# Attention scores of two heads beside each other on half arrays, three products a head, in place of two stacked whole-array products a head

## The chip, the cores and the metric

The kernel runs on one core of a Trainium2 chip. The metric is the device time of one execution in microseconds (us). The time before is 1629.16 us, the median of three runs (1628.31 to 1630.95). In the text, TensorE (PE in the profile, PEld for its weight loads) multiplies matrices, VectorE (DVE) and ScalarE (ACT) do elementwise work, GpSimd (POOL) helps, and SyncE (SP) issues most DMAs.

## The reference

A trunk of two layers over 512 latent tokens (a grid of 8 rows by 64 columns) and 256 context tokens, width 1024, all in float32. Each layer has an attention sub-layer and a SwiGLU sub-layer (hidden width 2816), each with a modulated RMSNorm ahead and a gated residual add behind. Layer 0 has four differential heads (each the difference of two softmaxes over all 768 keys) and eight neighbourhood heads (a window of the grid plus all context keys, with a bias). Layer 1 has 16 query heads on four key heads, with a window of 128 to each side, all context keys, and one learned sink logit a head. A head has 64 dimensions. What the change touches is the score computation, which in all of them has this core:

```python
s = jnp.einsum('bqhd,bnhd->bhqn', q, k).astype(jnp.float32) * (HEAD_DIM ** -0.5)
p = jax.nn.softmax(s, axis=-1)
...
o = jnp.einsum('bhqn,bnhd->bqhd', p.astype(v.dtype), v)
```

Context tokens go through the same layers but attend to context keys only; the second layer gives latent tokens alone.

## The kernel before

**Precision.** To keep float32 accuracy with TensorE's faster single-pass type (fp32r), every large operand is split into a high part, rounded to fp32r, and a low part, the rest. A projection (`mm3`, L205 to L210) makes three products: high by high, high by low, low by high. The projections, the two SwiGLU sub-layers and the scores work so; transposes and the product of probabilities and values (called PV here) use plain float32.

**Scores.** Two heads are handled as a pair; a projection leaves their 2 x 64 dimensions on 128 partitions. A head needs a sum over 64 partitions only, so `evac_pair` (L364) lays a head out on all 128: for head j it writes the high part to the head's own 64 partitions and the low part to the other 64. ScalarE makes the two high parts (L369), VectorE the two low ones (L372), each with 64 partitions. `swap_halves` (L386) makes by two DMAs a second copy `k2` of the keys with the halves exchanged. A whole-array product of q with `k1` then gives high by high plus low by low, and one with `k2` gives the two mixed terms: two products a head, each of 128 rows.

**Stages.** The differential heads are units u = 0 to 3 (`diff_steps`, L788), the neighbourhood heads units 4 to 7 (`na_steps`, L885). Each unit has four steps of 128 latent queries and one for the 256 context queries (`softmax_ctx`, L763). Score products are L804 and L805 (256 and 512 key columns), L912 and L914 (256 and 256) and, for context queries, L769 and L770 (256 each). The grouped-query stage of layer 1 has eight head pairs with four query blocks each (`gqa_step`, L1462); its products are L1477 (256 context keys) and L1479 (256 or 384 window keys). Behind the scores come, for each head, a minimum along the keys on VectorE (L806, L772, L915, L1481; the queries carry a factor of -0.125, so the minimum plays the maximum's part), the exponential on ScalarE (L808, L777, L922, L1486), a division by the sum (L782, L1494 and others), transposes on TensorE (L821, L935, L1503), copies out of PSUM, and PV (L825, L946, L1517). PV of the neighbourhood and of the grouped-query heads writes two heads to 64 columns of the array each, so that it shows as 128*64.

**PSUM.** It has eight banks. In layer 0's attention four belong to the score tiles (two tiles of two banks, `sps`), two to projections (`linp`) and two to transposes and PV (`tp`); in layer 1's attention four to scores, one to projections, three to the rest. A differential or a grouped-query step takes one score tile for each of its two heads; a neighbourhood step and a context step take one tile for both.

**Order.** `run_steps` (L406) issues a step's scores and softmax (`a`), then the transposes and PV of the step before (`b`), then a few fillers: projections for the next unit, the values, loads and low-rank sums for the modulation, and at the end first parts of the output projection. This is only a priority: the program is built with a scheduler that simulates the engines and orders each engine's instructions anew, earlier ones in the text first where they are ready. On the chip each engine runs its queue in that order. The keys' copies `k2` go through SP's queue, where the weight loads stand too (L131, L142), and `k2` has one buffer in layer 0, so that the swap of one unit waits for the last score products of the unit before.

Of the kernel before, what the change touches and what calls it, by code (L numbers as in the profile page):

```python
# [8 lines left out]
F32 = mybir.dt.float32  # L9
# [23 lines left out]
def f32(ap):  # L33
    return ap.bitcast(F32)
# [3 lines left out]
def tile_trunk(  # L38
# [325 lines left out]
    def evac_pair(dst, col, n, src, scale):  # L364

        c = slice(col, col + n)
        for j in range(2):
            a = slice(64 * j, 64 * j + 64)
            nc.scalar.activation(dst[a, j, c], src[a, :], AF.Copy, scale=scale)  # L369
        for j in range(2):  # L370
            a, o = slice(64 * j, 64 * j + 64), slice(64 - 64 * j, 128 - 64 * j)
            nc.vector.scalar_tensor_tensor(  # L372
                dst[o, j, c], src[a, :], scale, f32(dst[a, j, c]), op0=ALU.mult, op1=ALU.subtract
            )
# [220 lines left out]
    with ExitStack() as st:  # L595
        sps = st.enter_context(tc.tile_pool(name="a_s", bufs=2, space=PSUM, reuse_waits="tile"))
# [4 lines left out]
        sp2 = lambda shape=(P, 1024): sps.tile(list(shape), F32, tag="s", name="s")  # L601
# [30 lines left out]
        with ExitStack() as s0:  # L632
# [27 lines left out]
            psv = [sp2((P, 2, 512)) for _ in range(2)]  # L660
# [48 lines left out]
        def qk_tiles(u):  # L709
            units[u] = {  # L710
                "k": sp.tile([P, 2, NT], F32R, tag="k1", name="k1"),
                "k2": sp.tile([P, 2, NT], F32R, tag="k2", name="k2", bufs=1),
# [11 lines left out]
        def qk_c(u, key, w):  # L724
# [38 lines left out]
        def softmax_ctx(u):  # L763

            q, k1, k2 = (units[u][z] for z in ("q", "k", "k2"))
            s = sp2((P, 2, 2, 256))
            for c in range(2):
                for i in range(2):
                    nc.tensor.matmul(s[:, c, i, :], q[:, c, i * P : (i + 1) * P], k1[:, c, 0:256], start=True, stop=False)  # L769
                    nc.tensor.matmul(s[:, c, i, :], q[:, c, i * P : (i + 1) * P], k2[:, c, 0:256], start=False, stop=True)  # L770
            nm, rs = small("nm4", 4), small("rs4", 4)
            nc.vector.tensor_reduce(nm, s.rearrange("p a b n -> p (a b) n"), axis=AX.X, op=ALU.min)  # L772
# [15 lines left out]
        def diff_steps(u):  # L788
# [4 lines left out]
            def x_step(i):  # L793
                d = {}

                def a():
                    q, k1, k2 = (units[u][z] for z in ("q", "k", "k2"))
# [1106 lines left out]
```

## Time and profile before

| | |
|---|---|
| median of three runs | 1629.16 us |
| the profiled execution, its own time | 1634.54 us |
| its span, first to last instruction | 1632.7 us |
| mean granted TensorE clock | 0.992 |
| matmuls and weight loads | 10222 each |
| HBM read and written | 160.45 MB and 4.86 MB |

The profile shows one execution, and the lines that matter stand in the prediction. A line of a group gives the line of the kernel, the engine, the operation, the tiles it writes and reads, the shape, the count, then busy time in all and the mean duration of one in ns, then the idle time ahead of it and what ended it. A shape such as 128*64 behind a matmul is the part of the array it uses, rows by columns. In a timeline the first number is the start, the second the duration of the merged piece, and x2 says that two instructions of a kind were merged. Matmuls are pipelined, so that one's duration overlaps the next one's; the pace is read from start to start. In the sums by stage each engine has its busy time and count of instructions.

### The profile page before, as it was taken

Reading aid. Unit: us, or ns where it says so; the run is one execution under the profiler, and the core shown is the slowest. Engines: PE = TensorE matmul, PEld = TensorE weight load, DVE = VectorE, ACT = ScalarE, POOL = GpSimd, SP = SyncE. Lnnn points to the kernel's source line nnn. Section 1 sums busy time; section 2 is a strip of 40 time slices with the busy share of each in tenths; the row PEclk is TensorE's granted clock in tenths of the full one; section 3 lists DMA queues with packets and bytes.
Section 4 is the critical chain, followed back from the end, with each engine's and each line's share of the span. In section 5 each row is a group of like instructions: output and inputs, shape, how many; then the busy total and the mean of one; then the engine's idle time right before and its main releaser. Section 6 shows DMA issues by size and latency. Waiting matters only on the chain.

```text
span 1632.7 us, 26333 instructions
## 1 busy us (share of the span) xinstructions
PE 1569.6 (96%) x10222; PEld 1403.5 (86%) x10222; DVE 1255.6 (77%) x2157; ACT 747.0 (46%) x1324; POOL 267.0 (16%) x311
## 2 busy tenths in 40 slices
PE   5899998998999999999999999999999999999997
PEld 3798887886878899999999998887788899989897
DVE  4757698976688888978899867787665887869686
ACT  4446554555334532432424244456655542524344
POOL 2222222345010000010100011264322000000001
PEclk9999999999999999999999999999999999999999
DMA  9322244544235365576766753311010442323321
GB/s 343 98 57 85 89 149 129 186 139 132 72 109 154 95 183 158 152 197 168 195 180 169 211 134 95 104 53 40 14 40 27 152 132 66 125 82 104 117 78 52
DMA packets 69220, 198.48 MB, mean 122 GB/s; under 512 B 6900, under 2 KB 19348, under 8 KB 69096
## 3 DMA queue, kind: packets, MB, share of 16 engines
q1 hardware_dynamic: 59464, 164.40, 31.7%
q0 software_dynamic: 9056, 31.87, 9.1%
q8 instruction: 81, 1.33, 0.3%
q10 hardware_dynamic: 576, 0.52, 0.1%
q14 instruction: 43, 0.35, 0.1%
HBM read 160.45 MB, written 4.86 MB: 101 GB/s over the span
## 4 chain that ended last, share of the span: by engine, by line
PE 64%; DVE 7%; DMA 4%; issue 2%; ACT 2%; POOL 0%; DVEq 0%; SPq 0%; ACTq 0%; POOLq 0%
PE f L1272 5%; PE f L1274 5%; PE f L1273 5%; PE f L1685 4%; PE f L1684 4%; PE f L1683 4%; PE f L1313 3%; PE f L1314 3%; PE f L1315 3%; PE t L1517 2%; PE lin L207 2%; PE lin L208 2%; PE lin L209 2%; PE f L1737 2%; PE f L1736 2%; PE f L1738 2%
## 5 line engine op out<-in xcount | busy, mean ns | idle before, releaser
L196 ACT ACTIVATE wh<-raw 128x1024 fp32r<-128x1024 f32 (+1 forms) x96 | 92.3, 978 | 233.7 <-DVE raw L507 115.8
L207 PE MATMUL lin<-hb,wh 128*128 128x512 f32 (+1 forms) x456 | 162.8, 358 | 8.2 <-DVE q L372 2.2
L208 PE MATMUL lin<-hb,wh 128*128 128x512 f32 (+1 forms) x456 | 160.3, 352 | 0.5 <-DVE hb L197 0.4
L209 PE MATMUL lin<-hb,wl 128*128 128x512 f32 (+1 forms) x456 | 158.9, 348 | 0.0
L197 DVE TENSOR_TENSOR wl<-raw,wh 128x1024 fp32r<-128x1024 f32 (+1 forms) x96 | 106.8, 1119 | 34.9 <-ACT wh L196 32.9
L269 DVE SCALAR_TENSOR_TENSOR junk<-raw,tables 128x1024 bf16<-128x1024 f32 x80 | 97.7, 1222 | 20.2 <-DMA raw<-in_ada_wT_dram 19.9
L202 POOL DMA_DIRECT2D wl<-raw x39 | 34.1, 873 | 444.1 <-ACT wl L201 393.8
L207 PEld LDWEIGHTS lin<-hb,wh 128*128 128x128 f32 x456 | 86.4, 190 | 23.4 <-issue 4.5
L1313 PE MATMUL f<-g,wh 128*128 128x512 f32 (+1 forms) x304 | 102.8, 339 | 1.2 <-DVE q L1298 0.7
L1314 PE MATMUL f<-g,wh 128*128 128x512 f32 (+1 forms) x304 | 102.7, 339 | 0.0
L1684 PE MATMUL f<-hb,wh 128*128 128x256 f32 x360 | 101.7, 283 | 0.0
L1683 PE MATMUL f<-hb,wh 128*128 128x256 f32 x360 | 101.4, 283 | 0.0
L1685 PE MATMUL f<-hb,wl 128*128 128x256 f32 x360 | 101.2, 283 | 0.0
L1315 PE MATMUL f<-g,wl 128*128 128x256 f32 (+1 forms) x304 | 100.8, 336 | 0.0
L158 ACT CAST wh<-raw 128x1024 fp32r<-128x1024 f32 x61 | 63.9, 1047 | 77.9 <-PE lin L208 24.0
L1272 PE MATMUL f<-hb,wh 128*128 128x384 f32 x288 | 96.4, 335 | 0.9 <-ACT q L1259 0.9
L159 DVE TENSOR_TENSOR wl<-raw,wh 128x1024 fp32r<-128x1024 f32 x61 | 79.8, 1309 | 22.6 <-ACT wh L158 22.4
L208 PEld LDWEIGHTS lin<-hb,wh 128*128 128x128 f32 x456 | 86.7, 190 | 12.2 <-issue 0.9
L1274 PE MATMUL f<-hb,wl 128*128 128x384 f32 x288 | 96.3, 334 | 0.0
L1273 PE MATMUL f<-hb,wh 128*128 128x384 f32 x288 | 96.2, 334 | 0.0
L209 PEld LDWEIGHTS lin<-hb,wl 128*128 128x128 f32 x456 | 86.6, 190 | 10.4 <-issue 0.3
L339 POOL TENSOR_TENSOR ns_a<-ns_a,ns_s 128x256 f32<-128x256 f32 (+1 forms) x16 | 16.2, 1013 | 435.2 <-ACT ns_s L335 435.2
(395 smaller groups left out, 4948.7 us busy)
## 6 DMA issues: line engine op xcount, KB each, us to landing
raw<-in_w_dram SPq DMA_DIRECT2D x132, 512.0 KB, 3.7
raw<-in_ada_wT_dram SPq DMA_DIRECT2D x80, 512.0 KB, 4.2
wl<-raw POOLq DMA_DIRECT2D x39, 512.0 KB, 5.9
raw<-in_w_ab_dram SPq DMA_DIRECT2D x24, 512.0 KB, 4.2
raw<-in_ada_w_dram SPq DMA_DIRECT2D x16, 512.0 KB, 9.5
k<-k SPq DMA_DIRECT2D x16, 384.0 KB, 5.8
raw<-in_w_c_dram SPq DMA_DIRECT2D x12, 512.0 KB, 3.6
nb<-in_na_bias_dram POOLq DMA_DIRECT2D x16, 256.0 KB, 3.6
```

The lines of the kernel that those rows point to most:

```text
L207: nc.tensor.matmul(ps, wh(k), xh(k), start=k == 0, stop=False)
L208: nc.tensor.matmul(ps, wh(k), xl(k), start=False, stop=False)
L209: end = nc.tensor.matmul(ps, wl(k), xh(k), start=False, stop=k == n - 1)
L1272: nc.tensor.matmul(ps, wh(k), b[:, 0, :], start=k == 0, stop=False)
L1273: nc.tensor.matmul(ps, wh(k), b[:, 1, :], start=False, stop=False)
L1274: nc.tensor.matmul(ps, wl(k), b[:, 0, :], start=False, stop=k == 3)
L1313: nc.tensor.matmul(ps, hi, g[:, 0, cols[v]], start=first, stop=False)
L1314: nc.tensor.matmul(ps, hi, g[:, 1, cols[v]], start=False, stop=False)
L1315: nc.tensor.matmul(ps, lo, g[:, 0, cols[v]], start=False, stop=last)
L1683: nc.tensor.matmul(ps, wh(k), b[:, 0, :], start=k == 0, stop=False)
L1684: nc.tensor.matmul(ps, wh(k), b[:, 1, :], start=False, stop=False)
L1685: nc.tensor.matmul(ps, wl(k), b[:, 0, :], start=False, stop=k == 3)
```

## The change

- `evac_pair` writes the high part of both heads into one plane of the tile and the low part into another, all 128 partitions in one instruction on each engine. A head's high and low parts now lie on the same 64 partitions.
- A new helper, `scores`, takes three products for each head (high by high, high by low, low by high), each over the 64 partitions of that head. The two heads' products alternate: head 0 on rows 0 to 63 of the array, head 1 on rows 64 to 127. From the second product on, each is ordered behind the one before on TensorE and has a high priority in the scheduler.
- Layer 0 has no `k2` and no `swap_halves` any more. In layer 1 `k2` stays, because both query heads of a pair use the same key head, which must lie on both halves.
- The differential steps and the context steps of units 0 to 3 use one score tile of four banks for both heads (`sp4`); from unit 4 on the pool is replaced by the former two tiles of two banks (`sp2`). The grouped-query stage has one tile of four banks instead of two of two.
- A scratch tile of a later norm, which lay in `k2`'s place, has a tag of its own.

```diff
     def evac_pair(dst, col, n, src, scale):
         c = slice(col, col + n)
-        for j in range(2):
-            a = slice(64 * j, 64 * j + 64)
-            nc.scalar.activation(dst[a, j, c], src[a, :], AF.Copy, scale=scale)
-        for j in range(2):
-            a, o = slice(64 * j, 64 * j + 64), slice(64 - 64 * j, 128 - 64 * j)
-            nc.vector.scalar_tensor_tensor(
-                dst[o, j, c], src[a, :], scale, f32(dst[a, j, c]), op0=ALU.mult, op1=ALU.subtract
-            )
+        nc.scalar.activation(dst[:, 0, c], src, AF.Copy, scale=scale)
+        nc.vector.scalar_tensor_tensor(dst[:, 1, c], src, scale, f32(dst[:, 0, c]), op0=ALU.mult, op1=ALU.subtract)
+
+    def head(t, c):
+        return t[64 * c : 64 * c + 64]
+
+    def scores(*groups):
+        last = None
+        for outs, qs_, ks_ in groups:
+            for n, (a, b) in enumerate(((0, 0), (0, 1), (1, 0))):
+                for o, q, k in zip(outs, qs_, ks_):
+                    with tc.issue_after(last.ins) if last else nullcontext(), tc.high_priority() if last else nullcontext():
+                        last = nc.tensor.matmul(o, q(a), k(b), start=n == 0, stop=n == 2)
...
-        sps = st.enter_context(tc.tile_pool(name="a_s", bufs=2, space=PSUM, reuse_waits="tile"))
...
-        sp2 = lambda shape=(P, 1024): sps.tile(list(shape), F32, tag="s", name="s")
+        dst_ = st.enter_context(ExitStack())
+        dps = dst_.enter_context(tc.tile_pool(name="a_s", bufs=1, space=PSUM, reuse_waits="tile"))
+        sp4 = lambda: dps.tile([P, 2, 1024], F32, tag="s", name="s")
+        sps = []
+
+        def sp2(shape):
+            if not sps:
+                dst_.close()
+                sps.append(st.enter_context(tc.tile_pool(name="n_s", bufs=2, space=PSUM, reuse_waits="tile")))
+            return sps[0].tile(list(shape), F32, tag="s", name="s")
...
-                "k2": sp.tile([P, 2, NT], F32R, tag="k2", name="k2", bufs=1),
...
-            if key == "k":
-                swap_halves(units[u]["k2"], dst)
-            elif u >= 4:
+            if key == "q" and u >= 4:
...
-                    for c in range(2):
-                        s = sp2()
-                        for lo, n, at_ in ((256, 256, 0), (512, 512, 256)):
-                            nc.tensor.matmul(s[:, lo : lo + n], q[:, c, qc : qc + P], k1[:, c, at_ : at_ + n], start=True, stop=False)
-                            nc.tensor.matmul(s[:, lo : lo + n], q[:, c, qc : qc + P], k2[:, c, at_ : at_ + n], start=False, stop=True)
+                    both = sp4()
+                    both = [both[:, c] for c in range(2)]
+                    scores(*[(
+                        [s[:, lo : lo + n] for s in both],
+                        [lambda a, t=t: t[:, a, qc : qc + P] for t in qh],
+                        [lambda b, t=t, cs=slice(at_, at_ + n): t[:, b, cs] for t in kh],
+                    ) for lo, n, at_ in ((256, 256, 0), (512, 512, 256))])
+                    for c, s in enumerate(both):
...
-        sps = st.enter_context(tc.tile_pool(name="g_s", bufs=2, space=PSUM, reuse_waits="tile"))
+        sps = st.enter_context(tc.tile_pool(name="g_s", bufs=1, space=PSUM, reuse_waits="tile"))
...
-                for c in range(2):
-                    ql = q[:, c, i * P : (i + 1) * P]
-                    s = sps.tile([P, 1024], F32, tag="s", name="s")
-                    for n, k in ((0, k1), (1, k2)):
-                        nc.tensor.matmul(s[:, 256:512], ql, k[:, kv, 0:NC], start=(n == 0), stop=(n == 1))
-                    for n, k in ((0, k1), (1, k2)):
-                        nc.tensor.matmul(s[:, 512 : 512 + nk], ql, k[:, kv, NC + lo * P : NC + lo * P + nk], start=(n == 0), stop=(n == 1))
+                both = sps.tile([P, 2, 1024], F32, tag="s", name="s")
+                both = [both[:, c] for c in range(2)]
+                ql = [lambda a, t=head(q, c): t[:, a, i * P : (i + 1) * P] for c in range(2)]
+                kh = [head((k1 if kv % 2 == c else k2)[:, kv // 2], c) for c in range(2)]
+                cs = slice(NC + lo * P, NC + lo * P + nk)
+                scores(
+                    ([s[:, 256:512] for s in both], ql, [lambda b, t=t: t[:, b, 0:NC] for t in kh]),
+                    ([s[:, 512 : 512 + nk] for s in both], ql, [lambda b, t=t: t[:, b, cs] for t in kh]),
+                )
+                for c, s in enumerate(both):
```

The neighbourhood and the context steps change in the same way, with `scores` for their products.

More of the change, by code (lines that the diff above doesn't have):

```diff
@@ L1 @@
-from contextlib import ExitStack
+from contextlib import ExitStack, nullcontext
 import concourse.bass as bass
@@ L659, in tile_trunk @@
             psk, psq = linp(), linp()
-            psv = [sp2((P, 2, 512)) for _ in range(2)]
+            psv = sp4().rearrange("p c (t n) -> p c t n", t=2)
+            psv = [psv[:, t] for t in range(2)]
             wv = [tuple(wslice(t, 256) for t in wv)]
@@ L796, in a @@
                 def a():
-                    q, k1, k2 = (units[u][z] for z in ("q", "k", "k2"))
+                    qh, kh = ([head(units[u][z], c) for c in range(2)] for z in ("q", "k"))
                     qc = NC + i * P
@@ L1419, in k_x @@
             mm3(ps, *w, xh, xl)
-            evac_pair(k1[:, 2 * i : 2 * i + 2, :], NC, NX, rope_of(ps, gp), 1.0)
+            evac_pair(k1[:, i], NC, NX, rope_of(ps, gp), 1.0)
         def k_c(i, w):
```

44 lines of the change are left out of this document (22 added, 22 removed).

## Prediction

> **What bounds the kernel now.** I read the page first, then the sums by stage, then TensorE's timeline and the waits where the scores are computed.
>
> ```profile
> span 1632.7 us, 26333 instructions
> PE 1569.6 (96%) x10222; PEld 1403.5 (86%) x10222; DVE 1255.6 (77%) x2157; ACT 747.0 (46%) x1324; POOL 267.0 (16%) x311
> ...
> PE 64%; DVE 7%; DMA 4%; issue 2%; ACT 2%; POOL 0%; DVEq 0%; SPq 0%; ACTq 0%; POOLq 0%
> ```
>
> TensorE is busy for 96% of the span and makes 64% of the chain that ended last. The change lies in three stages, which by their first and last score products reach about from 75 to 257 us (differential heads), to 430 us (neighbourhood heads) and from 1055 to 1260 us (grouped-query heads); the sums over them:
>
> ```profile
> core 0: us, PE busy (x) PEld busy (x) DVE busy (x) ACT busy (x) POOL busy (x), PEclk, DMA share, GB/s
> 75.00:257.00 182.00, 175.26 (x1183) 159.20 (x1182) 133.80 (x213) 96.70 (x205) 38.64 (x38) 1.00 0.31 94
> 257.00:430.00 173.00, 164.18 (x1147) 138.85 (x1148) 129.58 (x248) 87.57 (x212) 67.94 (x94) 0.97 0.48 144
> 1055.00:1260.00 205.00, 200.09 (x1503) 161.68 (x1502) 141.00 (x329) 119.08 (x314) 77.00 (x82) 1.00 0.12 36
> ```
>
> TensorE idles 7, 9 and 5 us there; VectorE is at 74, 75 and 69%. So what counts is what TensorE's own queue gets longer or shorter, and only then its waits. Busy time of a matmul overlaps its neighbour's, so I take the pace from start to start:
>
> ```profile
> 1187.60 0.39 PE L209 MATMUL lin<-hb,wl 128*128 128x512 f32 x1
> 1187.83 0.39 PE L207 MATMUL lin<-hb,wh 128*128 128x512 f32 x1
> 1188.05 0.40 PE L1477 MATMUL s<-gk,gq 128*128 128x256 f32 x2
> 1188.29 0.40 PE L1479 MATMUL s<-gk,gq 128*128 128x256 f32 x2
> 1188.53 0.40 PE L208 MATMUL lin<-hb,wh 128*128 128x512 f32 x1
> 1188.76 0.40 PE L209 MATMUL lin<-hb,wl 128*128 128x512 f32 x1
> 1189.09 0.43 PE L1517 MATMUL t<-pt,gv 128*64 128x128 f32 x2
> 1189.45 0.50 PE L1477 MATMUL s<-gk,gq 128*128 128x256 f32 x2
> 1189.79 0.39 PE L1479 MATMUL s<-gk,gq 128*128 128x256 f32 x2
> 1190.11 1.09 PE L1517 MATMUL t<-pt,gv 128*64 128x128 f32 x14
> 1191.13 1.09 PE L1503 MATMUL t<-ident,p 128*128 128x128 f32 x8
> 1191.98 0.48 PE L207 MATMUL lin<-hb,wh 128*128 128x512 f32 x1
> ```
>
> Three prices come out. A product of 512 columns takes 0.23 us (1187.60 to 1187.83), one of 256 takes 0.12 (two from 1188.05 to 1188.29); 384 lies halfway, 0.175. The PV products (L1517) use half the array's columns each, two heads beside each other: 14 of them, the drain behind them included, start to next start 1.02 us, 73 ns each, while the eight whole-array transposes (L1503) with the same 128 moving columns take 0.85 us, 106 ns each. So two halves of the array do run at the same time, here halves of columns. And a change of that shape costs: L209 to L1517 takes 0.33 where 0.23 is the pace; the pair behind L1517 takes 0.34 (1189.45 to 1189.79) where 0.24 is the pace; L1479 to L1517 takes 0.32 instead of 0.24. I read 0.1 us for draining and another 0.1 for a first weight load that nothing covers, where the next operand is a large one.
>
> **The products.** Per 256 or 512 key columns, the two heads had four whole-array products; they get three pairs on halves of rows. If a pair runs as one product does, a quarter goes. Their counts:
>
> ```profile
> L1479 PE MATMUL s<-gk,gq 128*128 128x384 f32 x64 | 16.8, 341 | 0.0
> L912 PE MATMUL s<-k,q 128*128 128x256 f32 x64 | 15.5, 316 | 3.0 <-DMA k<-k 2.3 <-issue 0.4 <-ACT p L922 0.2
> L804 PE MATMUL s<-k,q 128*128 128x512 f32 x32 | 12.8, 399 | 0.0
> ...
> L769 PE MATMUL s<-k,q 128*128 128x256 f32 x32 | 8.7, 300 | 0.7 <-ACT p L808 0.6
> ```
>
> Each line stands for one of the two products of a head (L805, L914 and L770 are the second ones; L1477 and L1479 hold both), so there are 16 differential steps, 16 neighbourhood steps, 8 context steps and 32 grouped-query steps, half of these with 384 columns and half with 256. Before, a differential step is 4 x 0.12 + 4 x 0.23 = 1.40 us: a quarter is 0.35, times 16 is 5.6. A neighbourhood, context or short grouped-query step is 8 x 0.12 = 0.96: 0.24, times 40 is 9.6. A long grouped-query step is 0.48 + 0.70 = 1.18: 0.295, times 16 is 4.7. Sum **-19.9 us**. No row shows half arrays of rows: if the two halves ran one after the other it would be 12 products for 8, 79.6 x 0.5 = +39.8 us. I take the first, because the nearest row (L1517) shows two halves at once.
>
> **The changes of shape.** 72 score blocks (16 + 16 + 8 + 32) become stretches with another shape than the projections and transposes around them, two sides each. In the stretch above, one block lies between projections and the other between two PV runs, where a change is paid already; I take a third of the 104 sides of the 52 blocks beside PV work as paid, so 144 - 35 = 109 sides are new. At 0.2 us where a projection follows and 0.1 to 0.15 where a transpose with its smaller load does, I take 0.15: **+16 us**. Bounds: 0, if the row form needs no drain, and 144 x 0.2 = +29 if no block shares a side. "TensorEngine Tiling (Array Packing)" of the Trainium skill, section Tiling Modes, says that changing the tiling mode, not just the tile, drains TensorE. The gaps at L1517 agree for columns; the page gives no price, and no run here shows it for rows: by the rule the sum below stands, without it it falls by these 16 us.
>
> **The second copy of the keys.** In layer 0 every head pair sent its keys through two SP transfers to get them with halves swapped, and there is one such buffer: the transfer starts when the last scores of the pair before are done.
>
> ```profile
> 377.43 0.13 PE s L770
> ...
> 377.58 0.46 SPq L387
> ...
> 378.09 6.46 DMA k<-k
> ...
> 384.69 0.36 PE s L912
> ```
>
> ```profile
> PE lin L207 <- DVE q L372: 2.2, 1, 2.2
> ...
> PE s L805 <- DMA k<-k: 1.7, 1, 1.7
> ...
> PE s L912 <- DMA k<-k: 2.3, 2, 1.6
> ```
>
> Here the chain of waits runs through the copy, 377.58 to 384.69, while TensorE finds other work for part of it; its idle time that ended with the copy is 1.7 + 2.3 = 4.0 us. These waits go, and with them two places for each of eight head pairs in SP's queue, behind which weight loads stood. I take **-5 us**, between 4.0 and 7.1; what comes next there are the loads of the head outputs for the output projection. The four swaps of the grouped-query keys stay, of the same size.
>
> **Splitting whole.** evac_pair issues one instruction on ScalarE and one on VectorE instead of two each.
>
> ```profile
> core 0: us, ACT busy (x), PEclk, DMA share, GB/s
> 0.00:1633.00 1633.00, 45.65 (x88) 0.99 0.41 122
> ```
>
> ```profile
> core 0: us, DVE busy (x), PEclk, DMA share, GB/s
> 0.00:1633.00 1633.00, 54.30 (x88) 0.99 0.41 122
> ```
>
> These are L369 and L372. The columns per instruction stay, so half goes: 23 us of ScalarE, 27 of VectorE. TensorE covers nearly all of it; what waited for it is short (PE lin L207 <- DVE q L372, 2.2 us, in the waits above). I take **-2 us**, bounds 0 and -4.
>
> **One score tile for two.** The differential and the grouped-query stage had two score tiles in PSUM, one a head; now one holds both heads. The next block can begin only when both exponentials have read it; the neighbourhood stage keeps its two. A block at the head of TensorE's queue that waits holds back everything planned behind it, and the minimum on VectorE and the exponential on ScalarE behind that.
>
> ```profile
> 1155.26 0.48 PE L1477 MATMUL s<-gk,gq 128*128 128x256 f32 x2
> ...
> 1157.77 0.88 DVE L1481 CUSTOM_DVE_ANT_0 s<-s,gm,snk 128x640 f32<-128x640 f32 x1
> ...
> 1158.57 0.14 DVE L1481 DVE_READ_ACCUMULATOR2_ANT mx<- 128x1 f32 x1
> 1158.81 0.80 ACT L1486 ACTIVATE p<-s,mx 128x640 f32<-128x640 f32 x1
> 1159.15 0.48 PE L1477 MATMUL s<-gk,gq 128*128 128x256 f32 x2
> 1159.50 0.19 ACT L1486 ACTIVATION_READ_ACCUMULATOR p<-s,mx 128x1 f32 x1
> ```
>
> The second head's scores of two steps that follow each other stand at 1155.26 and 1159.15: a step without projections takes 3.9 us, and at 1159.15 the second head's block starts before the first head's exponential is read out. With one tile the circle is: three pairs of 256 and three of 384, 0.89 us; a change of shape, 0.2; two minima of 0.88 + 0.14, 2.04; the second exponential, 0.99; hand-over, some 0.2: 4.3 us. So a bare step grows by 0.4. The stage's 205 us are 6.4 us a step, so most steps carry projections that fill it; I reckon a third, 11 of 32, bare: **+5 us**. Bounds: 0, and all 32 steps, +14. In the differential stage (182 us for 20 blocks, 9 us a block) I take nothing.
>
> **The sum.** -19.9 + 16 - 5 - 2 + 5 = -5.9 us. The profiled execution took 1634.54 us with a span of 1632.7, 5.4 us above the median of 1629.16; the difference carries over: 1628.6 for such an execution, **1623.3 us** for the median. The ordering is made anew at build time, which may move it by some microseconds either way. 0.2%, what can be told from no change, is 3.3 us: 1625.9 to 1632.4.
>
> **The rivals.**
> *The row form changes without a drain.* The +16 goes: 1607 us. Against it stand the L1517 gaps; for it, that no row shows a half of rows. Chance 0.15.
> *The softmax circle takes over (slower).* Place: grouped-query steps behind the single tile. Other VectorE work that falls between the two minima (a pt copy, a weight split) lengthens the circle; from 0.6 us a step on, in all 32 steps, it is 19 us instead of 5, which eats the gain and more: -5.9 + 14 = +8, 1637 us. It decides as soon as it costs over 11 us. For it: VectorE at 69%. Against: 6.4 us a step is 2.1 us above the circle. Chance 0.20.
> *The halves overlap only in part, or not.* If a pair takes 4/3 of one product, nothing is saved: +14, 1643 us; with no overlap at all +53.8, 1683 us. This is also how it would look if other products came between the two of a pair. Chance 0.13. "TensorE: Matmul & The Clock Gate" of the Trainium skill, Measured speedup vs the span model, has 3.07 times for four row tiles, 77% of full; as an estimate from it, a pair would take 1.3 of one product, near the first of these. No run here shows that.
> *The saving and the changes of shape cancel,* with sides at 0.2 us: +22 for +16, sum 0: 1629 us. Chance 0.10.
>
> **How the numbers follow.** My forecast has 0.42, and by itself I give it 1615 to 1631: three quarters of it lie below 1625.9. Faster: 0.42 x 0.75 + 0.15 = 0.47. Within 0.2%: a fifth of the forecast, most of the last rival and a little of the softmax case, 0.21. Slower: 0.32. The range, 1605 to 1645, takes in the free change of shape, the softmax case and the partial overlap, and leaves out the serial halves and the tails.
>
> **What would show it.** The two products of a pair start some nanoseconds apart and pairs follow at 0.12 us for 256 columns; blocks of 12 products with 0.1 us extra on each side; no DMA k<-k in layer 0; 44 instructions on each of ScalarE and VectorE where 88 were; waits of score products for ACT p L808 and L1486. I am wrong if pairs follow at 0.2 us or more, or if TensorE idles over 15 us in the grouped-query stage.

## The result, and the profile after

The changed kernel took 1656.3 us (median of four runs, 1655.79 to 1659.42) against 1629.4 us for the kernel before in the same comparison: a ratio of 1.0168, 95% interval 1.0151 to 1.0186. It is slower by 27 us, where 6 us less was forecast, and above the upper end of the range. The profiled execution took 1655.79 us.

The page of the kernel after, the lines that answer to those of before:

```profile
span 1654.0 us, 26785 instructions
...
PE 1568.1 (95%) x10510; PEld 1384.9 (84%) x10510; DVE 1233.9 (75%) x2113; ACT 721.3 (44%) x1280; POOL 268.3 (16%) x311
...
PE 57%; DVE 6%; DMA 2%; ACT 2%; issue 2%; POOL 1%; DVEq 0%; POOLq 0%; ACTq 0%; SPq 0%
```

There are 288 matmuls more (72 blocks of 12 products where there were 8) and 44 instructions fewer on ScalarE and VectorE, as the diff says. TensorE's busy time is the same within 2 us, although the span is 21 us longer: the time went into idling. Where, the sums by stage say (the last stage is longer now, so its window is too):

```profile
core 0: us, PE busy (x) PEld busy (x) DVE busy (x) ACT busy (x) POOL busy (x), PEclk, DMA share, GB/s
75.00:257.00 182.00, 176.71 (x1273) 154.23 (x1272) 134.61 (x212) 91.51 (x198) 37.90 (x40) 1.00 0.27 85
257.00:430.00 173.00, 163.84 (x1230) 134.15 (x1228) 118.58 (x225) 79.10 (x191) 66.88 (x92) 0.98 0.38 120
1055.00:1285.00 230.00, 200.70 (x1638) 155.25 (x1637) 140.81 (x325) 115.19 (x308) 77.63 (x81) 0.99 0.10 30
```

In the grouped-query stage TensorE idles 29 us; before it was 5 (in a window 25 us shorter). The other two stages idle 5 and 9 us, where it was 7 and 9. From the last matmul of layer 0's SwiGLU to the last PV product of the stage it is 259.9 us, before 234.7: 25 of the 27 us. In the waits of that stage three things stand ahead of TensorE that were hardly there before:

```profile
PE s L382 <- ACT p L1508: 10.4, 14, 1.1
PE t L1525 <- POOL p L1516: 10.0, 16, 0.8
PE t L1539 <- ACT pt L1529: 3.5, 6, 0.9
PE t L1539 <- DVE pt L1527: 2.9, 12, 0.3
```

Score products (L382) wait for exponentials, transposes (L1525) for the scaled probabilities, PV products (L1539) for the copies of the transposed ones. All three hang on one circle: a step's scores, its minima, its exponentials, and only then the next step's scores. The timeline of all engines shows one turn of it (start, duration, engine, operation, and in brackets the idle time ahead and what ended it):

```profile
1154.25 1.15 PE L382 MATMUL s<-gk,gq 64*128 64x256 f32 x12 [0.66 <-ACT p L1508]
...
1155.44 0.89 DVE L1503 CUSTOM_DVE_ANT_0 s<-s,gm,snk 128x640 f32<-128x640 f32 x1 [0.50 <-PE s L382]
...
1156.25 0.14 DVE L1503 DVE_READ_ACCUMULATOR2_ANT mx<- 128x1 f32 x1
...
1156.71 0.59 ACT L1529 COPY pt<-t 128x512 f32<-128x512 f32 x1 [2.17 <-PE t L1525]
...
1157.19 0.80 ACT L1508 ACTIVATE p<-s,mx 128x640 f32<-128x640 f32 x1
...
1157.43 0.69 DVE L1527 COPY pt<-t 128x512 f32<-128x512 f32 x1 [1.04 <-PE t L1525]
...
1158.12 0.89 DVE L1503 CUSTOM_DVE_ANT_0 s<-s,gm,snk 128x640 f32<-128x640 f32 x1
...
1159.16 0.79 ACT L1508 ACTIVATE p<-s,mx 128x640 f32<-128x640 f32 x1 [0.63 <-DVE mx L1503]
...
1160.10 0.97 PE L382 MATMUL s<-gk,gq 64*128 64x256 f32 x12 [0.61 <-ACT p L1508]
```

The circle is 5.85 us (1154.25 to 1160.10) where the prediction reckoned 4.3. Block, minima and exponentials have about the lengths it gave them. What it had not is the hole between the two minima: the first is read out at 1156.39, the second begins at 1158.12, and VectorE stands idle for 1.04 us of that. The second head's scores have been ready since 1155.4. Then the copy of the step before (L1527), which the scheduler put there, runs until 1158.12; the first exponential, 1157.19 to 1158.08 with its readout, has ended just before. This step alone cannot tell which of the two the second minimum waited for. All steps together can: in each of the 32 steps of the stage the second minimum begins after the first exponential has ended, in 25 of them within 0.25 us of that end. The exponential in turn stood behind a copy (L1529) in ScalarE's queue. The groups of the minima name the wait too (L825 is the minimum of the differential heads, L1503 that of the grouped-query heads):

```profile
L825 DVE TENSOR_REDUCE nm<-s 128x1 f32<-128x768 f32 x32 | 30.5, 953 | 13.3 <-ACT p L827 8.8 <-PE s L382 4.3
L1503 DVE CUSTOM_DVE_ANT_0 s<-s,gm,snk 128x640 f32<-128x640 f32 x32 | 28.4, 888 | 8.1 <-PE s L382 4.5 <-ACT p L1508 3.3
...
L1503 DVE CUSTOM_DVE_ANT_0 s<-s,gm,snk 128x512 f32<-128x512 f32 x32 | 24.2, 756 | 12.8 <-PE s L382 6.9 <-ACT p L1508 5.8
```

Minima wait for exponentials (ACT p), 8.8 us in the differential stage and 9.1 in the grouped-query stage. They need none: the second minimum works on the second head's columns, the exponential reads the first head's. But both heads' columns are one tile now. In the kernel before, the same groups named the score products, and an exponential for 1.0 us only:

```profile
L806 DVE TENSOR_REDUCE nm<-s 128x1 f32<-128x768 f32 x32 | 30.2, 951 | 6.2 <-PE s L805 6.1
L1481 DVE CUSTOM_DVE_ANT_0 s<-s,gm,snk 128x640 f32<-128x640 f32 x32 | 28.3, 885 | 9.4 <-PE s L1479 9.4
L1481 DVE CUSTOM_DVE_ANT_0 s<-s,gm,snk 128x512 f32<-128x512 f32 x32 | 24.0, 752 | 12.2 <-PE s L1479 11.2 <-ACT p L1486 1.0
```

### The profile page after: what moved, and what is told of

Read it like the earlier page. It is cut to its first block, busy times and chain, and to the rows that moved or that the text cites. A ratio compares the mean times of both kernels' runs of the same rounds, so it can differ in the third digit from the quotient of the medians.

```text
span 1654.0 us, 26785 instructions
## 1 busy us (share of the span) xinstructions
PE 1568.1 (95%) x10510; PEld 1384.9 (84%) x10510; DVE 1233.9 (75%) x2113; ACT 721.3 (44%) x1280; POOL 268.3 (16%) x311
## 4 chain that ended last, share of the span: by engine, by line
PE 57%; DVE 6%; DMA 2%; ACT 2%; issue 2%; POOL 1%; DVEq 0%; POOLq 0%; ACTq 0%; SPq 0%
PE f L1290 5%; PE f L1292 5%; PE f L1291 5%; PE f L1707 4%; PE f L1706 4%; PE f L1705 4%; PE f L1332 3%; PE f L1331 3%; PE f L1333 3%; PE f L1759 2%; PE f L1760 2%; PE f L1758 2%; PE f L207 2%; PE f L208 2%; PE f L209 2%
## 5 line engine op out<-in xcount | busy, mean ns | idle before, releaser
L209 PE MATMUL lin<-hb,wl 128*128 128x512 f32 (+1 forms) x456 | 159.5, 350 | 0.0
L209 PEld LDWEIGHTS lin<-hb,wl 128*128 128x128 f32 x456 | 86.2, 189 | 12.2 <-issue 1.5
```

The costliest lines, as they stand in the source:

```text
L209: end = nc.tensor.matmul(ps, wl(k), xh(k), start=False, stop=k == n - 1)
```

## The experiments

Ratios are to the kernel before on the same chip (its median there was 1629.4 to 1632.5 us), with the 95% interval; 0.001 is 1.6 us, and kernels are compared with each other by their ratios. "Stage" is the time from the last matmul of layer 0's SwiGLU to the last PV product of the grouped-query heads, in each kernel's profiled execution.

| kernel | median us | ratio | stage us |
|---|---|---|---|
| before | 1629.4 to 1632.5 | 1 | 234.7 |
| after | 1656.3 | 1.0168 (1.0151 to 1.0186) | 259.9 |
| l0_only | 1634.1 | 1.0008 (1.0000 to 1.0017) | 235.0 |
| gqa_only | 1657.4 | 1.0152 (1.0138 to 1.0165) | 261.0 |
| one_tile_old_products | 1665.6 | 1.0204 (1.0188 to 1.0219) | 266.0 |
| copy_behind | 1670.3 | 1.0236 (1.0216 to 1.0256) | 275.4 |
| own_tiles_gqa | 1646.6 | 1.0091 (1.0078 to 1.0104) | 247.5 |
| own_tiles_all | 1642.1 | 1.0061 (1.0047 to 1.0074) | 248.6 |
| own_tiles_copy_behind | 1641.1 | 1.0056 (1.0041 to 1.0070) | 248.6 |
| own_tiles_l0 | 1625.7 | 0.9960 (0.9945 to 0.9976) | 234.9 |
| whole_blocks_all | 1638.4 | 1.0042 (1.0028 to 1.0056) | 246.3 |
| whole_blocks_l0 | 1626.9 | 0.9976 (0.9966 to 0.9986) | 234.7 |
| cut_before | 1615.6 | 0.9912 (0.9893 to 0.9931) | 219.2 |
| cut_two_tiles | 1619.7 | 0.9938 (0.9919 to 0.9956) | 222.6 |
| joined_old | 1643.2 | 1.0079 (1.0064 to 1.0095) | 247.4 |
| l0_copies | 1634.1 | 1.0027 (1.0013 to 1.0041) | 234.7 |

**Half of the change at a time.** l0_only has layer 0 as changed and the grouped-query stage as before; gqa_only is the other way round.

> Layer 0 as in the changed kernel, the grouped-query stage as before (stacked operands, two score tiles, evac in halves). Theory A (the loss is the single score tile of the grouped-query stage, layer 0 gains a little): 1624 to 1627 us, 2 to 5 below before. Rival B (blocks on half arrays with their changes of shape cost more than they save, everywhere): 1630 to 1640, since layer 0 holds 40 of the 72 blocks.

> Layer 0 as before, the grouped-query stage as in the changed kernel. Theory A: 1652 to 1660, the whole loss, PV of the stage ending about 25 us later. Rival B: 1638 to 1645, its share of the blocks, 32 of 72.

The grouped-query half loses nearly all of it, as theory A says. The layer 0 half, which by the prediction's terms was to bring some 8 us, brings nothing: there theory A missed, and the time lies in rival B's range, though own_tiles_l0 below shows another cause.

**One tile, old products.** The kernel before with one tile for the grouped-query scores of two heads, and the products of both heads ahead of the two minima; nothing else is changed:

```diff
-        sps = st.enter_context(tc.tile_pool(name="g_s", bufs=2, space=PSUM, reuse_waits="tile"))
+        sps = st.enter_context(tc.tile_pool(name="g_s", bufs=1, space=PSUM, reuse_waits="tile"))
...
-                for c in range(2):
+                both = sps.tile([P, 2, 1024], F32, tag="s", name="s")
+                both = [both[:, c] for c in range(2)]
+                for c, s in enumerate(both):
                     ql = q[:, c, i * P : (i + 1) * P]
-                    s = sps.tile([P, 1024], F32, tag="s", name="s")
...
+                for c, s in enumerate(both):
                     sv = s[:, 256 : 512 + nk]
```

> The kernel before, with one thing changed: both heads of a grouped-query step put their scores into one tile of four banks; products, operands and evac are the old ones. Theory A: most of the loss without any half-array product, 1643 to 1655. Rival B: 1629 to 1633, no more than the softmax circle of 0.4 us on 11 steps.

33 us slower, with the old products, and above the 1655 us that theory A gave. In the trace 31 of the 32 steps have their eight products in one block. So one tile for both heads, with the block that it brings, is enough to make the loss; the row form in its place is 6 us better in the stage (266.0 to 259.9).

**The copy out of the hole.** My first theory was that the scheduler's placing of the copy L1527 between the minima was the fault. copy_behind orders it behind the second minimum, which last_min holds:

```diff
...
-                        nc.vector.tensor_copy(pt[:, c, 0:4, :], t)
+                        with tc.issue_after(last_min[0].ins):
+                            nc.vector.tensor_copy(pt[:, c, 0:4, :], t)
```

> The changed kernel, with the VectorE copy of the transposed probabilities (pt of head 1) held behind the second minimum of the step that is being computed, so that it no longer stands between the two minima. Theory C (the order on VectorE's queue makes the circle long, since the copy waits for transposes that wait for GpSimd): bare steps fall from 5.8 us to 4.6 to 5.4, the time to 1636 to 1648. Theory A without C (the single tile alone, whatever the order): 1653 to 1659.

That theory fell: by the ratios 11 us more than the changed kernel, above the range of either theory. The copy had stood in a hole that was there anyway. The chain of waits of copy_behind shows it (start, duration, piece):

```profile
1153.40 0.90 ACT p L1510 x2
1154.32 0.89 DVE s L1505
1155.21 0.06 DVE mx L1505
1155.27 0.55 DVE pt L1530
1155.83 0.04 issue
1155.87 1.09 PE t L1542 x14
1156.96 1.08 PE s L382 x12
```

The second minimum (L1505, 1154.32) begins 0.02 us after the first exponential's two instructions end (1153.40 + 0.90). Behind it comes the copy, and only then the PV products, which wait for it, and the next block behind them in TensorE's queue. PV's waits for the copy, 2.9 us in the kernel after, were now these:

```profile
PE t L1542 <- DVE pt L1530: 23.4, 19, 1.9
```

**A tile for each head.** The same four banks, cut into two tiles of two; products and their order stay as in the changed kernel. own_tiles_gqa does so in the grouped-query stage, own_tiles_all in the differential and context steps too, own_tiles_copy_behind adds the order of copy_behind, and own_tiles_l0 has it in layer 0 alone, with the grouped-query stage of before.

```diff
-        sps = st.enter_context(tc.tile_pool(name="g_s", bufs=1, space=PSUM, reuse_waits="tile"))
+        sps = st.enter_context(tc.tile_pool(name="g_s", bufs=2, space=PSUM, reuse_waits="tile"))
...
-                both = sps.tile([P, 2, 1024], F32, tag="s", name="s")
-                both = [both[:, c] for c in range(2)]
+                both = [sps.tile([P, 1024], F32, tag="s", name="s") for _ in range(2)]
```

> The changed kernel with one edit: in the grouped-query stage each head of a pair gets a score tile of its own, two banks each, two of them in all; the space in PSUM, the products and their order stay. Theory D (the shared tile makes the second head's minimum wait for the first head's exponential, though they read different columns): that wait goes, bare steps go from 5.8 to 4.3-4.8 us, and the time to 1630-1645 us, at least 12 below the 1656 of the changed kernel. Rival E (pairing itself: a block needs both heads' exponentials of the step before, whatever the tiles are): the time stays at 1650 or more, and the score products go on waiting about 10 us for the exponentials in that stage.

> As own_tiles_gqa, and the differential and the context steps of layer 0 get a score tile for each head too. Theory D: the 16 differential steps lose the same wait; as layer 0 showed no loss against the kernel before, only 0 to 5 us come on top of own_tiles_gqa. Rival E: no difference from own_tiles_gqa over 2 us.

> As own_tiles_all, and in the grouped-query stage the copy of the first head's transposed probabilities stands behind the second head's minimum on VectorE, as in copy_behind. Theory D: with one tile the copy filled a wait that was there anyway; with two the minima run back to back, and the circle falls by the copy's 0.7 us in those steps where it stood between them: 0 to 12 us below own_tiles_all. Rival (the output products wait for the copy, as they did in copy_behind): the same as own_tiles_all or up to 15 us above it.

> Layer 0 changed, with a score tile for each head in the differential and context steps; the grouped-query stage as in the kernel before. l0_only, with one tile for two heads there, stood at 1.0008 of the kernel before. Theory D: the wait in the 16 differential steps, up to 0.9 us each, costs part of it: 0.995 to 0.999 of the kernel before. Rival F (the layer's score blocks are covered by TensorE's other work, and changes of shape eat what the pairs save): 0.999 to 1.002.

The minima of own_tiles_all (L813 differential, L1490 grouped-query):

```profile
L813 DVE TENSOR_REDUCE nm<-s 128x1 f32<-128x768 f32 x32 | 29.5, 949 | 6.1 <-PE s L382 6.1
L1490 DVE CUSTOM_DVE_ANT_0 s<-s,gm,snk 128x640 f32<-128x640 f32 x32 | 27.1, 889 | 10.1 <-PE s L382 10.1
...
L1490 DVE CUSTOM_DVE_ANT_0 s<-s,gm,snk 128x512 f32<-128x512 f32 x32 | 22.8, 755 | 8.2 <-PE s L382 8.2
```

Only the tiles were changed, and every wait of a minimum for an exponential is gone: in all 32 steps of own_tiles_gqa the second minimum begins 0.9 to 1.9 us before the first exponential ends. The grouped-query stage gets 12.4 us shorter (259.9 to 247.5), and in own_tiles_all steps without projections now take 4.0 to 5.0 us (the blocks at 1149.64, 1154.59 and 1158.60). That is theory D, though the time of own_tiles_gqa, 1646.6, ends just outside its 1645 and is 9.7 below the changed kernel's median, 12.5 by the ratios. In layer 0, own tiles turn l0_only's 1.0008 into 0.9960: this kernel beats both. Moving the copy now makes no difference that can be told.

The stage is still 13 us above the kernel before. In own_tiles_all TensorE hardly idles any more; in the same 195 us of before and of it (columns as in the sums by stage above):

```profile
1040.00:1235.00 195.00, 191.06 (x1397) 153.44 (x1396) 139.96 (x321) 116.34 (x301) 77.52 (x80) 1.00 0.18 52
```

```profile
1040.00:1235.00 195.00, 188.93 (x1436) 141.81 (x1435) 125.71 (x289) 99.45 (x267) 74.06 (x76) 0.99 0.16 48
```

3.9 us idle before, 6.1 in own_tiles_all. So there TensorE's queue itself got longer. The scheduler often sends a block's first product ahead alone, since the first head's tile comes free first. In 23 of the 32 blocks (not 25, as the expectation of whole_blocks_all has it) other matmuls follow it:

```profile
1097.86 0.38 PE L382 MATMUL s<-gk,gq 64*128 64x256 f32 x1
1098.17 0.50 PE L207 MATMUL lin<-hb,wh 128*128 128x512 f32 x1
```

It occupies TensorE for 0.31 us, start to start, and the other eleven enter again later.

**Blocks kept whole.** The pair begins with the head whose tile comes free last, so that the block's first product does the waiting for all twelve. Each head has a fixed tile, and the order of minima and exponentials is fixed. The lines show the edit against the changed kernel.

```diff
-                for o, q, k in zip(outs, qs_, ks_):
+                for o, q, k in zip(outs[::-1], qs_[::-1], ks_[::-1]):
...
-                both = sps.tile([P, 2, 1024], F32, tag="s", name="s")
-                both = [both[:, c] for c in range(2)]
+                both = [sps.tile([P, 1024], F32, tag=f"s{c}", name="s") for c in range(2)]
...
-                    nc.vector.tensor_tensor_reduce(
...
+                    with chained(chain, 0):
+                        mn = nc.vector.tensor_tensor_reduce(
...
```

> own_tiles_all with its score blocks kept whole: each head has one fixed tile, the first head's minimum and exponential come first, and each pair starts with the second head's product, so that the first product waits for the later of the two exponentials and the other eleven wait for nothing. In own_tiles_all 25 of the 32 grouped-query blocks and 9 of the 16 differential ones had their first product alone (0.31 us instead of 0.12, other shapes behind it, and a second entry for the rest). Theory G (the split costs about 0.3 us a block): 7 us less in the grouped-query stage and 3 in layer 0: 1628 to 1636 us. Rival E (the step's circle needs both exponentials, so a block kept whole only starts later): 1640 to 1650.

> own_tiles_l0 (layer 0 changed, a tile for each head; the grouped-query stage as in the kernel before) with the 16 differential blocks kept whole in the same way. Theory G: 1 to 3 us below own_tiles_l0, 0.994 to 0.996 of the kernel before. Rival E: 0.996 to 0.999.

No block of the grouped-query stage is split now, but the stage is only 2.3 us shorter than in own_tiles_all, not 7, and the intervals of the two ratios overlap; 1638.4 us lies between the ranges of the two theories. Theory G had the price of the split: TensorE's work in the stage, idle time left out, falls from 238.2 to 227.9 us. But it forgot why the product went ahead. The block starts later, and the transposes and PV products behind it wait: idle time in the stage rises from 10.4 to 18.5 us. TensorE idles 15.3 of the same 195 us, and the longest waits are these:

```profile
PE t L1529 <- POOL p L1520: 6.8, 13, 1.4
PE t L1543 <- DVE pt L1531: 4.1, 13, 0.6
...
1040.00:1235.00 195.00, 179.72 (x1484) 136.89 (x1484) 130.18 (x303) 105.20 (x287) 74.69 (x78) 1.00 0.14 40
```

In layer 0 whole blocks show no gain over own_tiles_l0 (0.9976 and 0.9960, the intervals overlap), as rival E said.

**Room for two steps.** If the loss is the circle from step to step, two buffers should break it. PSUM has no room for them with 640 columns a head; with 512 it has. So cut_before is the kernel before with fewer window keys: it leaves out the third block of 128 in the steps that have one. cut_two_tiles is the changed kernel with the same block left out, and with two buffers of the shared tile. The first line below is in both, the others are in cut_two_tiles alone.

```diff
+            hi = lo + 1
...
-        sps = st.enter_context(tc.tile_pool(name="g_s", bufs=1, space=PSUM, reuse_waits="tile"))
+        sps = st.enter_context(tc.tile_pool(name="g_s", bufs=2, space=PSUM, reuse_waits="tile"))
...
-                both = sps.tile([P, 2, 1024], F32, tag="s", name="s")
+                both = sps.tile([P, 2, 512], F32, tag="s", name="s")
...
```

> The kernel before, but every grouped-query step takes only two window blocks (256 window keys): the third block of the two middle query blocks is left out of the scores, the softmax and the output product. It is the measure for cut_two_tiles. All theories: below the kernel before by 16 steps of some 0.23 us of score products, 0.3 of transposes and output products and a shorter softmax, 8 to 20 us in all.

> The changed kernel with the same third window block left out in every grouped-query step; the scores of both heads then fit into two banks, so there are two buffers of the shared tile, and a block no longer waits for the exponentials of the step before but of the one before that. Theory D (the loss is the step-to-step circle behind the shared tile, not the row form): no more than 3 us above cut_before, and down to 8 below it by the quarter of 30.7 us of products less the changes of shape. Rival H (the row form itself, its changes of shape and the longer single stretches, makes the loss): 10 us or more above cut_before.

4.1 us above cut_before, 3.4 in the stage: between the two theories, far nearer to D's end than to H's. TensorE hardly waits in cut_two_tiles, 1.6 us of 195:

```profile
1040.00:1235.00 195.00, 193.38 (x1517) 147.56 (x1516) 134.68 (x318) 104.84 (x282) 75.19 (x82) 1.00 0.17 49
```

The shared tile's wait is still there: in 25 of the 32 steps the second minimum begins within 0.25 us after the first exponential's end, as in the changed kernel. With a second buffer the next block does not wait for that, and it costs little: it takes the wait and the single buffer together to make the loss. The cut kernel with one buffer was not run, so how much the shorter steps have to do with it stays open.

The pair also prices the row form, with the two heads in one block that it forces. Summed over the stage, from each matmul's start to the next one's, by kind, idle time included: score products 38.9 to 29.0 us, PV 39.4 to 44.8, transposes 29.6 to 34.8, all others 111.2 to 114.0. The scores save 9.9 and everything else pays 13.3 (unrounded), which leaves the 3.4. TensorE changes shape, from one matmul to the next, 168 times instead of 93. If all of the 13.3 is put down to the 75 new changes, each costs 0.18 us. TensorE's timeline of one block:

```profile
1125.71 0.40 PE L209 MATMUL lin<-hb,wl 128*128 128x512 f32 x1
1126.04 0.98 PE L382 MATMUL s<-gk,gq 64*128 64x256 f32 x12
1126.95 1.09 PE L1540 MATMUL t<-pt,gv 128*64 128x128 f32 x14
```

From L209 to the block 0.33 us where its pace is 0.23; the block, with its entry and its drain, 0.91 for six pairs of 256 columns.

**Two heads in one block, with the old products.** What was left in the stage with own tiles, 12 to 14 us over the kernel before, could come from the row form or from what it forces: both heads of a step in one block. joined_old is the kernel before with the eight old products of a step bound into one block in the way of whole_blocks_all; no product, copy or tile has another size.

```diff
...
+                both = [sps.tile([P, 1024], F32, tag=f"s{c}", name="s") for c in range(2)]
...
+                for lo_, n_, at_ in ((256, 256, 0), (512, nk, NC + lo * P)):
                     for n, k in ((0, k1), (1, k2)):
+                        for c in (1, 0):
+                            with tc.issue_after(last.ins) if last else nullcontext(), tc.high_priority() if last else nullcontext():
...
```

> The kernel before, with one edit in the grouped-query stage: the eight old products of a step's two heads are one block, as the pairs force it, the second head's product first in each place, each head on a fixed tile of its own, the first head's minimum and exponential first, as in whole_blocks_all. No product, copy or tile is changed in size. Theory I (binding two heads makes the loss that is left: the block waits for the later exponential, both minima come late and the transposes wait for the scaled probabilities): 8 to 18 us above the kernel before, with 8 us or more of waits of the transposes and output products in that stage. Rival J (with tiles of their own the binding costs little, and the 11 us between whole_blocks_all and whole_blocks_l0 are changes of shape): less than 5 us above the kernel before, down to 2 below.

Theory I holds: 12.9 us slower by the ratio, the stage 12.7 us longer. The waits of transposes and PV products that the profile names sum to some 7 us, a little less than the 8 expected, and score products wait another 3.0 for exponentials; TensorE idles 10.9 of the 195 us. Here are the two longest of these waits and the sums:

```profile
PE t L1523 <- DVE pt L1511: 4.5, 9, 1.0
PE s L1479 <- ACT p L1491: 3.0, 3, 1.2
...
1040.00:1235.00 195.00, 184.11 (x1331) 146.87 (x1329) 130.85 (x303) 109.75 (x284) 75.53 (x76) 0.99 0.16 46
```

Idle time in the stage grows from 7.1 to 14.5 us; the other 5.3 us show as no idle time, and what they are made of stays open. The fixed tiles and the fixed order of minima and exponentials were not run by themselves. The timeline shows the block behind the second exponential, as theory I has it:

```profile
1154.70 0.67 ACT L1491 ACTIVATE p<-s,mx 128x512 f32<-128x512 f32 x1
1155.27 0.20 ACT L1491 ACTIVATION_READ_ACCUMULATOR p<-s,mx 128x1 f32 x1
...
1155.52 1.21 PE L1479 MATMUL s<-gk,gq 128*128 128x256 f32 x8 [1.22 <-ACT p L1491]
```

In the kernel before, one head's block runs while the other head's exponential does. Bound together, TensorE has no score product to give the softmax while ScalarE works on the last one.

**The copy of the keys put back.** l0_copies is own_tiles_l0 with the two SP transfers of each head pair's keys, old size, one buffer, read by the middle one of each three products:

```diff
+                "k2": sp.tile([P, 2, NT], F32R, tag="k2", name="k2", bufs=1),
...
+            if key == "k":
+                straight(units[u]["k2"], dst)
...
-                [lambda b, t=t: t[:, b, 0:256] for t in kh],
+                [lambda b, t=t, t2=t2: (t2 if b else t)[:, b, 0:256] for t, t2 in zip(kh, k2h)],
```

> own_tiles_l0 with the two SP transfers of each head pair's keys put back, of the old size and into one buffer as before, as a plain copy that the middle product of each three reads. Theory (the term of the prediction for the second copy of the keys, 5 us between 4.0 and 7.1, holds): 4 to 7 us above own_tiles_l0, 0.9985 to 1.0005 of the kernel before, and waits of score products for a DMA of some 4 us. Rival (the copy was hidden, its 4.0 us of waits give way to other waits): within 2 us of own_tiles_l0 and whole_blocks_l0, 0.995 to 0.998.

It costs more than either side expected: 1.0027 against 0.9960 (11 us) or against 0.9976 (8 us). TensorE's idle time in layer 0's attention, 60 to 430 us, in the order before, own_tiles_l0, l0_copies:

```profile
60.00:430.00 370.00, 352.55 (x2431) 310.35 (x2430) 275.92 (x477) 192.39 (x429) 115.06 (x140) 0.99 0.40 118
```

```profile
60.00:430.00 370.00, 361.61 (x2637) 306.66 (x2638) 258.83 (x449) 177.38 (x400) 113.97 (x137) 1.00 0.33 103
```

```profile
60.00:430.00 370.00, 353.24 (x2578) 298.96 (x2578) 253.18 (x442) 174.06 (x396) 112.28 (x136) 1.00 0.40 117
```

17.4, 8.4 and 16.8 us: with the copies back, the idle time is back. But of the 8.4 us only 2.7 carry the copy's name:

```profile
PE s L394 <- DMA k<-k: 2.7, 3, 1.2
```

## Why the prediction was wrong, point by point

**The products: right.** The two products of a pair start 2 to 17 ns apart (six pairs of the block at 1126.04 us above), and pairs of 256 columns follow each other at 0.12 us. In layer 0 the score products went from 55.8 us, start to start, to 44.4 in own_tiles_l0: 11.4 us less, and the prediction's terms for layer 0 sum to 11.4 (5.6 and 24 x 0.24). That the sums agree to the tenth is luck: 4.6 of the 55.8 us are idle time behind a product, and of the 44.4 none are. The pace of the pairs is what shows it.

**The changes of shape: about right in price, wrong in number.** 0.15 us each was taken; the cut pair gives 0.18, if all that it pays is changes of shape. "TensorEngine Tiling (Array Packing)" of the Trainium skill, section Tiling Modes, has a drain at a change of mode. For rows, which no row showed before, the traces now agree, with the 0.33 us from L209 to L382. The number was reckoned from the blocks, 109 new changes. In the trace of the changed kernel there are 59 more than before (270 against 211): 71 more in layer 0's attention, but 12 fewer in the grouped-query stage (115 against 127), where the score products stand in 32 whole blocks and stood in 60 pieces before.

**The second copy of the keys: too small.** 5 us, between 4.0 and 7.1, was taken from the waits that name the copy; putting it back cost 8 to 11. The waits that name a transfer are not all that it cost; the rest came back as waits under other names, which the trace does not tie to it.

**Splitting whole: right where it shows.** The 88 instructions of VectorE, 54.30 us, became 44 with 25.95, and ScalarE's 88 with 45.65 us became 44 with 22.52. No run tells what of it reached the time.

**One score tile for two: the step that failed.** It said "With one tile the circle is: three pairs of 256 and three of 384, 0.89 us; a change of shape, 0.2; two minima of 0.88 + 0.14, 2.04" and so on to 4.3 us, in 11 of 32 steps, +5 us. The sum put the two minima back to back. With a shared tile the second waits for the first exponential, which is itself late behind a copy on ScalarE: a hole of 1.73 us in the step shown, and a circle of 5.85. The stage became 25.2 us longer, and three steps of the experiments lead there: 12.7 for two heads in one block (234.7 to 247.4, joined_old), -1.1 for the row form with its changes of shape (247.4 to 246.3, whole_blocks_all), 13.6 for the shared tile, together with the block's old order (246.3 to 259.9). The tile by itself is worth 12.4 (own_tiles_gqa). These are parts along one way, and they do not simply add: the old products in one tile cost 31.3 in the stage. The middle step is not clear of 0, since two kernels with the same grouped-query stage, own_tiles_gqa and own_tiles_all, differ by as much. It is near what the prediction's own terms give for this stage, products -8.6 (16 x 0.24 and 16 x 0.295) and 48 sides at 0.15, +7.2, but that is luck: whole_blocks_all has only 12 more changes of shape than joined_old (117 against 105). Its work without idle time is 5.0 us shorter (232.9 to 227.9), and 4.0 us more of idle time (14.5 to 18.5) took most of that back. What the prediction missed is that pairing takes away the overlap of one head's block with the other's softmax, and that sharing a tile then orders two engines that share no data.

**Nothing in the differential stage: wrong too.** The shared tile cost layer 0 its gain: 1.0008 with it, 0.9960 and 0.9976 without. With own tiles layer 0 came out 4 to 6.5 us faster; the prediction's terms for it (-11.4 for products, 61 sides at 0.15, -5 for the copies, -1) make it -8.

**The rival** *The softmax circle takes over* had the place and the direction, but not the cause: it named "Other VectorE work that falls between the two minima", and copy_behind shows that the copy there was not what the second minimum waited for. Its price, 0.6 us in each of 32 steps, was too small as well: 25.2 us in the stage are 0.8 a step. The prediction had named its own refutation: TensorE idling over 15 us in the grouped-query stage. It idles 29.

**What stays open.** Why a shared tile makes one engine's read wait for another's is not shown by a trace; that the tile is the condition is. What a shared tile would cost with the first exponential not behind a copy in ScalarE's queue was not run. And why the copies of the keys cost 8 to 11 us when their waits name less than 3 is only shown as idle time that comes and goes with them; the wait for the data and the places in SP's queue were not tried apart.

## What to carry to other kernels

Before two heads, or any two independent pieces, are put into one block or one buffer, walk through one whole step and ask which engine worked on one piece while another had the other; that overlap is part of the price, and no product's time shows it. Give each piece a tile of its own even where the memory is the same, since here a tile was also a unit of waiting; in the cut pair, with a second buffer, a shared tile cost little. And where a circle's sum puts two operations back to back, look for what the second of them would have to wait for: a busy share, here VectorE's 69%, says nothing about that.

## What the runs showed of the hardware that was not expected

- Two products on halves of rows run fully beside each other: six pairs of 256 columns, entry and drain included, took 0.91 us, and 0.72 is the pace of six whole-array products. The Trainium skill's measured figure in "TensorE: Matmul & The Clock Gate", section Measured speedup vs the span model, is 3.07 times for four row tiles, 77% of full. For two no such loss shows here: pairs follow each other at 0.10 to 0.12 us.
- A single half-array product between whole-array ones took 0.31 us of TensorE's time where its pace in a row of them is 0.12 a pair.
